# Strided attention: Q cast to bf16 on GpSimd and transposed in 32x32 blocks on VectorE, in place of TensorE transposes and ScalarE copies

## Chip, cores, metric

The kernel runs on one core of one Trainium2 chip. The metric is the device time of one execution in microseconds. Every kernel was run several times; medians are quoted with the lowest and highest run. All runs quoted were in the fast state. Ratios are the mean time of one kernel's fast runs over the mean of the other's fast runs of the same rounds, so not quite the ratio of the medians quoted beside them. The profile's span starts and ends inside the execution and is about 1.8 us shorter than the time (128.5 us for a run of 130.28).

## The reference

Shapes are batch 8, heads 12, sequence 1024, head size 64, float32. Every query attends only to the 16 keys and values at positions 0, 64, 128, ...:

```python
attend = np.arange(0, seq, stride)              # 16 positions
scores  = einsum('bhqd,bhkd->bhqk', q, K[:, :, attend]) / sqrt(64)
weights = exp(scores - max) ; weights /= weights.sum() + 1e-10
result  = einsum('bhqk,bhkd->bhqd', weights, V[:, :, attend])
```

There is little arithmetic. All of Q (25.2 MB) is read and an output of the same size is written; with the few rows of K and V that makes 51.12 MB of transfers.

## The kernel before

The 96 (batch, head) pairs are worked on in 24 groups of four. Per group: one 1 MB load of Q, 16 TensorE transposes, two ScalarE copies of the transposed Q to SBUF, four score matmuls that run side by side on 32 columns of the array each (four of about 0.39 us in 0.40 us together), two exps, eight small matmuls for the sums, a reciprocal, eight output matmuls, four VectorE products that normalise, one 1 MB store. Loads run up to 11 groups ahead.

```python
def transposes(g, x):                       # x = 0, 1
    ps = psum_qt.tile([P, 8, P], BF16, ...)
    for i in range(8):
        nc.tensor.transpose(ps[:, i], <high halves of qn[g], 128 columns>, identity)
    nc.scalar.copy(qt[g][:, x], ps)
def scores(g):
    for j in range(4):
        nc.tensor.matmul(sc[32*j:32*j+32], lhsT=kt[:, 32*j:32*j+32], rhs=<qt[g]>,
                         start=True, stop=True, tile_position=(0, 32*j))
    # ... two exps on ScalarE into w[g]
# ... sums(g): 8 matmuls and a reciprocal; outputs(g, c): 2 matmuls and a product
for g in range(NG):
    sums(g); outputs(g, 0); outputs(g, 1)
    if g + 1 < NG: scores(g + 1)
    outputs(g, 2)
    if g + 2 < NG: transposes(g + 2, 0)
    outputs(g, 3)
    if g + 2 < NG: transposes(g + 2, 1)
    store(g)
    if g + QBUFS < NG: load(g + QBUFS)      # QBUFS = 11
```

The softmax here doesn't subtract the row's maximum and nothing guards it: scores larger than these inputs give would overflow.

## Time and profile before

| | before |
|---|---|
| time, median of 3 (lowest, highest) | 130.45 us (130.32, 130.61) |
| DMA queue, share of 16 engines' span | 96.3% |
| bytes per group / measured rate | 2.1 MB / about 420 GB/s = 5.0 us |
| period of the compute loop | 3.93 us per group |
| last store issued | 114.3 us |

These are lines of the page of before: busy time by engine, the DMA row in 40 slices (tenths) with GB/s below it, the DMA queues (packets, MB, share of 16 engines), the chain that ended last, and the costliest groups of instructions (busy us, mean ns of one, idle before and its cause).

```profile
span 128.5 us, 2215 instructions
...
PE 69.4 (54%) x880; PEld 51.1 (40%) x880; DVE 83.7 (65%) x144; ACT 86.3 (67%) x103; POOL 5.1 (4%) x23
...
DMA  2999989999899899999999999999998999999980
GB/s 57 351 398 418 449 367 490 388 423 439 339 421 487 357 441 439 413 434 449 383 467 426 393 459 428 393 469 421 405 469 357 416 434 416 421 428 421 434 337 23
...
q1 hardware_dynamic: 7712, 51.12, 96.3%
q8 instruction: 7, 0.11, 0.4%
q14 instruction: 3, 0.02, 0.0%
...
ACT 60%; PE 13%; DVE 5%; DMA 3%; POOL 3%; issue 2%; ACTq 1%; DVEq 0%; POOLq 0%
...
L243 DVE TENSOR_TENSOR out_sb<-o_ps,rec 128x512 f32<-128x512 f32 x96 | 63.3, 688 | 15.3 <-PE o_ps L238 12.9
L198 ACT COPY qt<-qt_ps 128x1024 bf16<-128x1024 bf16 x48 | 46.2, 1015 | 5.2 <-PE qt_ps L193 4.7
L218 ACT ACTIVATE w<-sc 64x512 bf16<-64x512 f32 x48 | 35.4, 737 | 13.2 <-PE sc L206 12.9
...
L193 PE MATMUL qt_ps<-identity,qn 128*128 128x128 bf16 x384 | 30.7, 227 | 0.2 <-ACT qt L198 0.2
...
L206 PE MATMUL sc<-qt,k_t 128*32 128x512 bf16 x96 | 9.8, 395 | 24.5 <-ACT qt L198 24.5
...
```

The chain of waits names ScalarE, and it is right about the compute loop: copy, copy, score matmuls, exp, exp, one after the other. But that loop is not what ends the run. The DMA row reads 8 or 9 from the third slice to the third last. The queue of the sync engine tells how the run ends; the columns are who waited for what, total us, times, longest:

```profile
...
SPq L34 <- DVE out_sb L243: 20.0, 12, 3.3
...
SPq L307 <- DMA out_dram<-out_sb: 12.6, 1, 12.6
...
```

After the last store has been issued the kernel waits 12.6 us for stores to land.

The last microseconds in stretches (window, length, busy us of the engines with counts, TensorE clock, DMA share, GB/s):

```profile
...
core 0: us, PE busy (x) PEld busy (x) DVE busy (x) ACT busy (x) POOL busy (x), PEclk, DMA share, GB/s
...
90.00:110.00 20.00, 13.42 (x182) 9.83 (x179) 15.32 (x26) 17.33 (x21) 0.00 (x0) 1.00 1.00 418
...
118.00:122.00 4.00, 0.00 (x0) 0.00 (x0) 0.00 (x0) 0.00 (x0) 0.00 (x0) 0.50 1.01 426
...
124.00:125.00 1.00, 0.00 (x0) 0.00 (x0) 0.00 (x0) 0.00 (x0) 0.00 (x0) 0.50 0.61 254
125.00:126.00 1.00, 0.00 (x0) 0.00 (x0) 0.00 (x0) 0.00 (x0) 0.00 (x0) 0.50 0.26 107
...
```

### The profile page before, as it was taken

To read this page: it belongs to the slowest core of one execution; us is meant where nothing else is said; L and a number is where in the kernel's file an instruction comes from. 1 tells how busy PE (TensorE), PEld (TensorE's weight loads), DVE (VectorE), ACT (ScalarE), POOL (GpSimd) and SP (SyncE) were. 2 spreads that over 40 slices of the span, in tenths; PEclk is the share of its full clock that TensorE was granted. 3 is DMA by queue.
4 is the path that set the end of the run, shared out by engine and by line. 5 is a ranking of instruction groups with operands and counts; after the bars stand their busy time and mean duration, and the time that the engine had idled before them with its cause. 6 is when DMAs were issued, how large, how long until landed. Compare 5 with 4: busy or idle time off the path is not lost.

```text
span 128.5 us, 2215 instructions
## 1 busy us (share of the span) xinstructions
PE 69.4 (54%) x880; PEld 51.1 (40%) x880; DVE 83.7 (65%) x144; ACT 86.3 (67%) x103; POOL 5.1 (4%) x23
## 2 busy tenths in 40 slices
PE   0071665975656866558766578665687655510000
PEld 0040542754445654445544456443465444300000
DVE  6229963787677777787777877877877778750000
ACT  2163294988889888898888898888988888400000
POOL 4470000000000000000000000000000000000000
PEclk9999997799999999999999999999999999955555
DMA  2999989999899899999999999999998999999980
GB/s 57 351 398 418 449 367 490 388 423 439 339 421 487 357 441 439 413 434 449 383 467 426 393 459 428 393 469 421 405 469 357 416 434 416 421 428 421 434 337 23
DMA packets 7722, 51.26 MB, mean 399 GB/s; under 512 B 3872, under 2 KB 3872, under 8 KB 3872
## 3 DMA queue, kind: packets, MB, share of 16 engines
q1 hardware_dynamic: 7712, 51.12, 96.3%
q8 instruction: 7, 0.11, 0.4%
q14 instruction: 3, 0.02, 0.0%
HBM read 25.95 MB, written 25.17 MB: 398 GB/s over the span
## 4 chain that ended last, share of the span: by engine, by line
ACT 60%; PE 13%; DVE 5%; DMA 3%; POOL 3%; issue 2%; ACTq 1%; DVEq 0%; POOLq 0%
ACT qt L198 34%; ACT w L218 26%; PE sc L206 8%; DVE v_bd L180 3%; DMA k_raw<-in_K_dram 3%; PE qt_ps L193 2%; PE o_ps L238 2%; DVE out_sb L243 1%; POOL k_dup L116 1%; POOL perm_v L120 1%; PE sm L227 1%; POOL v_bf L124 1%; ACTq L307 1%; DVEq L307 0%; PE vp L175 0%
## 5 line engine op out<-in xcount | busy, mean ns | idle before, releaser
L243 DVE TENSOR_TENSOR out_sb<-o_ps,rec 128x512 f32<-128x512 f32 x96 | 63.3, 688 | 15.3 <-PE o_ps L238 12.9
L198 ACT COPY qt<-qt_ps 128x1024 bf16<-128x1024 bf16 x48 | 46.2, 1015 | 5.2 <-PE qt_ps L193 4.7
L218 ACT ACTIVATE w<-sc 64x512 bf16<-64x512 f32 x48 | 35.4, 737 | 13.2 <-PE sc L206 12.9
L238 PE MATMUL o_ps<-v_bd,w 128*128 128x256 bf16 x192 | 33.4, 278 | 0.6 <-DVE out_sb L243 0.6
L193 PE MATMUL qt_ps<-identity,qn 128*128 128x128 bf16 x384 | 30.7, 227 | 0.2 <-ACT qt L198 0.2
L193 PEld LDWEIGHTS <-qn 128*128 128x128 bf16 x384 | 27.0, 102 | 3.9 <-issue 2.6
L206 PE MATMUL sc<-qt,k_t 128*32 128x512 bf16 x96 | 9.8, 395 | 24.5 <-ACT qt L198 24.5
L238 PEld LDWEIGHTS <-w 128*128 128x128 bf16 x192 | 14.3, 98 | 6.9 <-issue 6.2
L206 PEld LDWEIGHTS <-k_t 128*32 128x32 bf16 x96 | 4.4, 93 | 29.3 <-issue 29.2
L231 DVE RECIPROCAL rec<-sm 128x32 f32<-128x32 f32 x24 | 8.6, 358 | 9.0 <-PE sm L227 9.0
L227 PE MATMUL sm<-s_sel,w 128*128 128x4 bf16 x192 | 8.5, 166 | 6.9 <-ACT w L218 6.9
L227 PEld LDWEIGHTS <-w 128*128 128x128 bf16 x192 | 6.4, 96 | 11.0 <-ACT w L218 11.0
L180 DVE TENSOR_SCALAR v_bd<-vp,mask 128x384 bf16<-128x384 f32 x16 | 8.5, 608 | 0.1
L166 ACT CAST k_t<-kp 64x512 bf16<-64x512 f32 x6 | 3.5, 579 | 3.6 <-PE kp L160 3.5
L160 PE MATMUL kp<-perm_k,k_dup 128*128 128x128 bf16 x12 | 1.5, 312 | 6.7 <-POOL k_dup L116 6.7
L175 PE MATMUL vp<-v_bf,perm_v 128*128 128x384 bf16 x4 | 1.8, 490 | 4.6 <-DVE v_bd L180 4.1
L160 PEld LDWEIGHTS <-k_dup 128*128 128x128 bf16 x12 | 1.2, 145 | 6.7 <-POOL k_dup L116 6.7
L138 DVE TENSOR_SCALAR slot_i<-iota_p 128x1 int16<-128x1 int16 x1 | 0.2, 156 | 4.7 <-POOL iota_p L136 4.7
L166 ACT ACT_TABLE_LOAD x1 | 1.3, 1283 | 2.5 <-DVE k_t L127 2.5
L127 DVE MEMSET k_t<- 128x1536 uint32 x1 | 1.3, 1338 | 1.1 <-PEq L293 1.1
L175 PEld LDWEIGHTS <-perm_v 128*128 128x128 bf16 x4 | 0.5, 127 | 3.7 <-issue 3.7
L116 POOL CAST k_dup<-k_raw 128x768 bf16<-128x768 f32 x2 | 1.6, 827 | 3.0 <-DMA k_raw<-in_K_dram 3.0
(15 smaller groups left out, 6.0 us busy)
## 6 DMA issues: line engine op xcount, KB each, us to landing
qn<-in_Q_dram SPq DMA_DIRECT2D x24, 1024.0 KB, 19.0
out_dram<-out_sb SPq DMA_DIRECT2D x24, 1024.0 KB, 19.5
k_raw<-in_K_dram SPq DMA_DIRECT2D x1, 384.0 KB, 4.3
v_raw<-in_V_dram SPq DMA_DIRECT2D x1, 384.0 KB, 5.4
```

The source lines that it names most:

```text
L116: nc.gpsimd.tensor_copy(out=k_dup[:, :, e], in_=k_raw)
L160: nc.tensor.matmul(kp[:, i], lhsT=k_dup[:, 4 * n + i].rearrange("p e d -> p (e d)"), rhs=pk, start=True, stop=True,)
L166: nc.scalar.copy(k_t[h, 4 * n : 4 * n + 4, :, :, e].rearrange("p n c s k -> p (n c s) k"), kp[h].rearrange("p n c s k -> p (n c s) k"),)
L180: nc.vector.tensor_scalar(out=v_bd[:, 6 * n : 6 * n + 6, c, s], in0=vp, scalar1=mask[:, s : s + 1], scalar2=None, op0=ALU.mult,)
L193: nc.tensor.transpose(ps[:, i], _ap_with(qb, [qb.ap[0], [2, P]], extra_offset=(8 * x + i) * 2 * P + 1), identity,)
L198: nc.scalar.copy(qt[g][:, x], ps)
L206: nc.tensor.matmul(sc[32 * j : 32 * j + 32], lhsT=kt[:, 32 * j : 32 * j + 32], rhs=_ap_with(q, [q.ap[0], [P, 8], [8 * P, 2], [1, 32]], ext ...
L218: nc.scalar.activation(out=_ap_with(wa, [wa.ap[0], [P, 8], [1, 2], [2, 32]], extra_offset=64 * a), in_=sc[64 * a : 64 * a + 64].rearrange( ...
L227: nc.tensor.matmul(sm[:, :, i], lhsT=wt[g][:, i], rhs=s_sel, start=True, stop=True)
L231: nc.vector.reciprocal(rec[g], sm.rearrange("p b i e -> p b (i e)"))
L238: nc.tensor.matmul(ps[:, :, i], lhsT=wt[g][:, 2 * c + i], rhs=v_bd[:, g // 2, g % 2].rearrange("p s d -> p (s d)"), start=True, stop=True,)
L243: nc.vector.tensor_tensor(out=out_sb[g][:, :, 4 * c : 4 * c + 4], in0=ps.rearrange("p b i (e d) -> p b (i e) d", e=2), in1=rec[g][:, :, 4 ...
```

## The change

The intent is to relieve TensorE and ScalarE. GpSimd casts Q to bf16; VectorE transposes it as 32x32 blocks of 32-bit words, each a pair of bf16 values; the scores then contract over (head, d pair) with the full height of the array, in four accumulating matmuls against keys set in zeros. The values are multiplied with a head mask per group on GpSimd, the keys are prepared in three portions, two of them inside the loop. K, Q0, V are loaded in that order, and the first two loads of Q have 128 rows of 8 KB in place of 32 of 32 KB.

```diff
-    QBUFS = 11
+    QBUFS = 10
-        _copy(nc, qn[g], <Q of group g in 32 rows>)
+        n = P if g < 2 else 32
+        _copy(nc, qn[g], <Q of group g in n rows>)
 # ... K, V, Q0, Q1 ... becomes K, Q0, V, Q1 ...
-    nc.vector.memset(k_t, 0.0)
+    nc.vector.memset(k_t[:, 0:8], 0.0)
+    nc.gpsimd.memset(k_t[:, 8:NG], 0.0)
-    def transposes(g, x): ...            # 8 PE transposes, 1 ScalarE copy, twice per group
+    def cast(g):
+        nc.gpsimd.tensor_copy(out=qb[g], in_=qn[g])
+    def transpose(g):
+        nc.vector.transpose(qt[g].bitcast(I32), qb[g].bitcast(I32))
+    def values(g):
+        nc.gpsimd.tensor_tensor(out=vb[g], in0=mask, in1=<v_rep>, op=ALU.mult)
     def scores(g):
-        for j in range(4): matmul(sc[32*j:32*j+32], ..., tile_position=(0, 32*j))
+        for e in range(2):
+            for f in range(2):
+                nc.tensor.matmul(sc, lhsT=k_t[:, g, f, NK*(1-e):NK*(1-e)+P],
+                                 rhs=<qt[g], every second column>, start=e+f == 0, stop=e+f == 2)
+    keys(0); cast(0); transpose(0); scores(0); value_rows(); values(0)
+    cast(1); transpose(1); values(1); cast(2)
     for g in range(NG):
+        if g + 2 < NG: transpose(g + 2)
         sums(g) ... outputs(g, 3)        # scores(g + 1) stays between outputs 1 and 2
+        if g + 2 < NG: values(g + 2)
+        if g + 3 < NG: cast(g + 3)
+        if g in (2, 4): keys(g // 2)
         store(g)
 # ... cuts: tiles and pools, keys(), value_rows(), set-up
```

More of the change, by code (lines that the diff above doesn't have):

```diff
@@ L14 @@
 I16 = mybir.dt.int16
+I32 = mybir.dt.int32
 AF = mybir.ActivationFunctionType
@@ L68 @@
     SD = S * D
+    KW = P + NK
     assert B * H == NG * HG and S == 1024 and D == 64 and NK == 16
-    QBUFS = 11
+    QBUFS = 10
     OBUFS = 9
@@ L75 @@
     out_pool = ctx.enter_context(tc.tile_pool(name="outsb", bufs=OBUFS))
+    qb_pool = ctx.enter_context(tc.tile_pool(name="qb", bufs=2))
     qt_pool = ctx.enter_context(tc.tile_pool(name="qt", bufs=2))
+    vb_pool = ctx.enter_context(tc.tile_pool(name="vb", bufs=3))
     rec_pool = ctx.enter_context(tc.tile_pool(name="rec", bufs=2))
-    psum_qt = ctx.enter_context(tc.tile_pool(name="pqt", bufs=2, space=bass.MemoryType.PSUM))
     psum_sc = ctx.enter_context(tc.tile_pool(name="psc", bufs=2, space=bass.MemoryType.PSUM))
-    psum_o = ctx.enter_context(tc.tile_pool(name="po", bufs=3, space=bass.MemoryType.PSUM))
-    psum_s = ctx.enter_context(tc.tile_pool(name="psm", bufs=1, space=bass.MemoryType.PSUM))
+    psum_o = ctx.enter_context(tc.tile_pool(name="po", bufs=4, space=bass.MemoryType.PSUM))
+    psum_s = ctx.enter_context(tc.tile_pool(name="psm", bufs=2, space=bass.MemoryType.PSUM))
     ctx.enter_context(tc.manual_schedule())
@@ L88 @@
     kv_src = [[stride * D, P], [2 * HG * SD, NC], [1, D]]
-    nc.sync.dma_start(k_raw, _ap_with(K, kv_src))
-    nc.sync.dma_start(v_raw, _ap_with(V, kv_src))
     qn = {}
@@ L95, in load @@
         qn[g] = qn_pool.tile([P, 32 * D], FP32, name="qn", tag="qn")
-        _copy(
-            nc, qn[g], _ap_with(Q, [[HG * SD // 32, 32], [1, HG * SD // 32]], g * HG * SD)
-        )
-    for g in range(QBUFS):
+        n = P if g < 2 else 32
+        _copy(nc, qn[g], _ap_with(Q, [[HG * SD // n, n], [1, HG * SD // n]], g * HG * SD))
+    nc.sync.dma_start(k_raw, _ap_with(K, kv_src))
+    load(0)
+    nc.sync.dma_start(v_raw, _ap_with(V, kv_src))
+    for g in range(1, QBUFS):
         load(g)
@@ L110 @@
     perm_v = const.tile([P, 2, 2, 2, 2, NK], BF16, name="perm_v")
+    iota_p = const.tile([P, 1], I16, name="iota_p")
+    nc.gpsimd.iota(iota_p, pattern=[[0, 1]], base=0, channel_multiplier=1)
+    col4 = const.tile([P, 4], I16, name="col4")
+    nc.gpsimd.iota(col4, pattern=[[1, 4]], base=0, channel_multiplier=0)
     for c in range(2):
@@ L113 @@
             nc.gpsimd.tensor_copy(out=perm_k[:, c, a], in_=id_v[:, c, :, a])
-    k_dup = const.tile([P, NC, 2, D], BF16, name="k_dup")
-    for e in range(2):
-        nc.gpsimd.tensor_copy(out=k_dup[:, :, e], in_=k_raw)
     for c in range(2):
@@ L122 @@
                 )
-    v_bf = const.tile([P, NC, D], BF16, name="v_bf")
-    nc.gpsimd.tensor_copy(out=v_bf, in_=v_raw)
-    k_t = const.tile([P, NC, 2, 4, 2, NK], BF16, name="k_t")
-    nc.vector.memset(k_t, 0.0)
+    k_t = const.tile([P, NG, 2, KW], BF16, name="k_t")
+    nc.vector.memset(k_t[:, 0:8], 0.0)
     w_bufs = []
@@ L132 @@
         w_bufs.append(w)
-    iota_p = const.tile([P, 1], I16, name="iota_p")
-    nc.gpsimd.iota(iota_p, pattern=[[0, 1]], base=0, channel_multiplier=1)
+    nc.gpsimd.memset(k_t[:, 8:NG], 0.0)
     slot_i = const.tile([P, 1], I16, name="slot_i")
@@ L143 @@
     nc.vector.tensor_copy(out=slot_f, in_=slot_i)
-    col4 = const.tile([P, 4], I16, name="col4")
-    nc.gpsimd.iota(col4, pattern=[[1, 4]], base=0, channel_multiplier=0)
     s_sel = const.tile([P, 4], BF16, name="s_sel")
@@ L149 @@
     )
-    mask = const.tile([P, 4], FP32, name="mask")
-    nc.vector.tensor_scalar(
-        out=mask, in0=col4, scalar1=slot_f, scalar2=None, op0=ALU.is_equal
-    )
-    pk = perm_k.rearrange("p c a b k -> p (c a b k)")
-    for n in range(NC // 4):
-        kp = psum_o.tile([P, 4, 2, 4, NK], FP32, name="kp", tag="o")
-        for i in range(4):
-            nc.tensor.matmul(
-                kp[:, i], lhsT=k_dup[:, 4 * n + i].rearrange("p e d -> p (e d)"),
-                rhs=pk, start=True, stop=True,
-            )
-        for e in range(2):
-            h = slice(64 * e, 64 * e + 64)
+    slot_m = const.tile([P, 4], FP32, name="slot_m")
@@ new lines, with keys @@
+    nc.vector.tensor_copy(out=slot_m, in_=s_sel)
+    mask = const.tile([P, 4, D], BF16, name="mask")
+    nc.vector.tensor_copy(out=mask, in_=s_sel.unsqueeze(2).to_broadcast([P, 4, D]))
+    k_m = const.tile([P, NC, 2, 4, 32], BF16, name="k_m")
+    v_bf = const.tile([P, NC, D], BF16, name="v_bf")
+    v_rep = const.tile([P, NC, 2, D], BF16, name="v_rep")
+    def keys(m):
+        kr = k_raw[:, 4 * m : 4 * m + 4].rearrange("p n (q f) -> p n f q", f=2)
+        for h in range(4):
+            nc.vector.tensor_scalar(
+                out=k_m[:, 4 * m : 4 * m + 4, :, h], in0=kr,
+                scalar1=slot_m[:, h : h + 1], scalar2=None, op0=ALU.mult,
+            )
+        for u in range(2):
+            kp = psum_o.tile([P, 2, 2, 2, 4 * NK], FP32, name="kp", tag="o")
+            for i in range(2):
+                for f in range(2):
+                    nc.tensor.matmul(
+                        kp[:, i, :, f],
+                        lhsT=k_m[:, 4 * m + 2 * u + i, f].rearrange("p h q -> p (h q)"),
+                        rhs=perm_k.rearrange("p c a b k -> p c (a b k)"),
+                        start=True, stop=True,
+                    )
+            g0 = 8 * m + 4 * u
+            dst = k_t[:, g0 : g0 + 4]
@@ L166 @@
             nc.scalar.copy(
-                k_t[h, 4 * n : 4 * n + 4, :, :, e].rearrange("p n c s k -> p (n c s) k"),
-                kp[h].rearrange("p n c s k -> p (n c s) k"),
-            )
-    v_bd = const.tile([P, NC, 2, 4, D], BF16, name="v_bd")
-    for n in range(2):
-        for c in range(2):
-            vp = psum_sc.tile([P, NC // 2, D], FP32, name="vp", tag="sc")
-            nc.tensor.matmul(
-                vp, lhsT=perm_v[:, c].rearrange("p a b e k -> p (a b e k)"),
-                rhs=v_bf[:, 6 * n : 6 * n + 6], start=True, stop=True,
-            )
-            for s in range(4):
-                nc.vector.tensor_scalar(
-                    out=v_bd[:, 6 * n : 6 * n + 6, c, s], in0=vp,
-                    scalar1=mask[:, s : s + 1], scalar2=None, op0=ALU.mult,
-                )
@@ L185 @@
-    qt, wt, rec, out_sb = {}, {}, {}, {}
-    def transposes(g, x):
-        if x == 0:
-            qt[g] = qt_pool.tile([P, 2, 8, P], BF16, name="qt", tag="qt")
-        ps = psum_qt.tile([P, 8, P], BF16, name="qt_ps", tag="qt_ps")
-        qb = qn[g].bitcast(BF16)
-        for i in range(8):
-            nc.tensor.transpose(
-                ps[:, i],
-                _ap_with(qb, [qb.ap[0], [2, P]], extra_offset=(8 * x + i) * 2 * P + 1),
-                identity,
-            )
-        nc.scalar.copy(qt[g][:, x], ps)
+                _ap_with(dst, [dst.ap[0], [KW, 8], [32, 4], [1, NK]], extra_offset=NK),
@@ new lines, in keys, with value_rows @@
+                kp.rearrange("p i c f (s k) -> p (i c f) s k", s=4),
+            )
+    def value_rows():
+        nc.vector.tensor_copy(out=v_bf, in_=v_raw)
+        for n in range(2):
+            for c in range(2):
+                vp = psum_sc.tile([P, NC // 2, D], FP32, name="vp", tag="sc")
+                nc.tensor.matmul(
+                    vp, lhsT=perm_v[:, c].rearrange("p a b e k -> p (a b e k)"),
+                    rhs=v_bf[:, 6 * n : 6 * n + 6], start=True, stop=True,
+                )
+                nc.vector.tensor_copy(out=v_rep[:, 6 * n : 6 * n + 6, c], in_=vp)
@@ new lines @@
+    qb, qt, wt, vb, rec, out_sb = {}, {}, {}, {}, {}, {}
+    def values(g):
+        vb[g] = vb_pool.tile([P, 4, D], BF16, name="vb", tag="vb")
+        nc.gpsimd.tensor_tensor(
+            out=vb[g], in0=mask,
+            in1=v_rep[:, g // 2, g % 2].unsqueeze(1).to_broadcast([P, 4, D]),
+            op=ALU.mult,
+        )
+    def cast(g):
+        qb[g] = qb_pool.tile([P, 32 * D], BF16, name="qb", tag="qb")
+        nc.gpsimd.tensor_copy(out=qb[g], in_=qn[g])
+    def transpose(g):
+        qt[g] = qt_pool.tile([P, 32 * D], BF16, name="qt", tag="qt")
+        nc.vector.transpose(qt[g].bitcast(I32), qb[g].bitcast(I32))
@@ L202, in scores @@
         q = qt[g]
-        kt = k_t[:, g // 2, g % 2].rearrange("p s e k -> p (s e k)")
-        for j in range(4):
-            a, b = divmod(j, 2)
-            nc.tensor.matmul(
-                sc[32 * j : 32 * j + 32],
-                lhsT=kt[:, 32 * j : 32 * j + 32],
-                rhs=_ap_with(
-                    q, [q.ap[0], [P, 8], [8 * P, 2], [1, 32]],
-                    extra_offset=32 * (2 * b + a),
-                ),
-                start=True, stop=True, tile_position=(0, 32 * j),
-            )
+        for e in range(2):
+            for f in range(2):
+                nc.tensor.matmul(
+                    sc, lhsT=k_t[:, g, f, NK * (1 - e) : NK * (1 - e) + P],
+                    rhs=_ap_with(
+                        q, [q.ap[0], [2 * D, 8], [16 * D, 2], [2, 32]],
+                        extra_offset=D * e + f,
+                    ),
+                    start=e + f == 0, stop=e + f == 2,
+                )
         w = wt[g] = w_bufs[g % 3]
@@ L239, in outputs @@
                 ps[:, :, i], lhsT=wt[g][:, 2 * c + i],
-                rhs=v_bd[:, g // 2, g % 2].rearrange("p s d -> p (s d)"),
+                rhs=vb[g].rearrange("p s d -> p (s d)"),
                 start=True, stop=True,
@@ L256, in store @@
         )
-    for g in range(2):
-        for x in range(2):
-            transposes(g, x)
+    keys(0)
+    cast(0)
+    transpose(0)
     scores(0)
+    value_rows()
+    values(0)
+    cast(1)
+    transpose(1)
+    values(1)
+    cast(2)
     for g in range(NG):
+        if g + 2 < NG:
+            transpose(g + 2)
         sums(g)
@@ L268 @@
         outputs(g, 2)
-        if g + 2 < NG:
-            transposes(g + 2, 0)
         outputs(g, 3)
         if g + 2 < NG:
-            transposes(g + 2, 1)
+            values(g + 2)
+        if g + 3 < NG:
+            cast(g + 3)
+        if g in (2, 4):
+            keys(g // 2)
         store(g)
```

## The prediction

> **What bounds the kernel now.** The transfers. The page's DMA row reads 9 tenths from the third slice to the third last; the hardware DMA queue is busy for 96.3% of the 128.5 us span while moving 51.12 MB, and the table of windows shows DMA share 0.99 to 1.03 and 418 to 434 GB/s from 28 us to 124 us. Idle: the first 2.3 us and the last 2. The chain of waits names ScalarE instead (qt copy 34%, exp 26%): that is the compute loop, which steps every 3.93 us per group of four heads (qt copies 1.94, score matmuls 0.42, exps 1.49). But a group moves 2.1 MB, which at 420 GB/s takes 5.0 us. So the loop is faster. It ends at 114.2 us and the last 12.6 us are a wait for stores to drain.
>
> **What the change does, per group.**
> - TensorE loses 16 transposes (about 1.2 us) and gains a full-height score: four serial 512-column matmuls, [...]in place of four concurrent ones (0.40).
> - ScalarE loses the two qt copies (1.94) and keeps 1.49 of exp.
> - GpSimd gains the cast of 128x2048. The 128x768 cast took 827 ns, so an estimate is 2.2 us[...].
> - VectorE gains one block transpose of 128x1024 32-bit pairs. [...]With the reciprocal (0.36) and four products (2.48 together when nothing holds them, as at the end of before) VectorE has about 4.1 us per group and becomes the loop's limit.
> - Setup shrinks: the first store should be issued near 16 to 17 us in place of 25.2.
>
> **Contention.** [...]I expect little; the products should stay at 0.69 us.
>
> **On the critical path.** Almost nothing. Bytes and packets are the same (two loads become 8 KB packets). The new loop, some 4.1 to 4.4 us, is still under the 5.0 of the transfers and starts 8 us earlier, so compute ends near 112 to 120 us and the rest drains. One Q buffer less matters little. Gains can come only from small dips of the DMA between 20 and 28 us (share 0.93), half a microsecond at most.
>
> **Prediction:** 130.2 us, 8 in 10 between 129.0 and 132.3. Chances: faster by over 2% 0.05, within 2% 0.82, slower by over 2% 0.13.
>
> **What would show it.** DMA busy 95 to 97%, windows between 30 and 120 us at 415 to 430 GB/s; [...]cast near 2.2 us; products 0.69 us; ScalarE busy about 40 us, VectorE about 105 us; the first store near 16 us; the chain of waits passing to VectorE and DMA; final wait for stores 8 to 14 us.
>
> **What would make it wrong.** If the loop's period exceeds about 4.5 us ([...]casts and VectorE blocking one another), compute ends after 125 us, the DMA runs dry and the time becomes period times 24 plus about 20: 139 us at 4.9. It would be faster only if the transfers themselves became faster, which I don't expect.

To follow the forecast's sums: VectorE came to about 4.1 us per group, and the loop's 4.1 to 4.4 us and VectorE's 105 us rest on it. Its terms 0.36 and 2.48 us are from the trace of before.

## The result, and the profile after

| | before | after |
|---|---|---|
| time, median of 4 (lowest, highest) | 130.38 us (130.2, 130.61) | 129.76 us (129.49, 129.87) |
| ratio, 95% interval | | 0.9948 (0.9926 to 0.997) |
| first store issued | 25.2 us | 23.6 us |
| last store issued | 114.3 us | 120.0 us |
| TensorE instructions in the program | 1,762 | 1,018 |

The change gains half a percent (the interval lies below 1, and well within 2%). This is the page after, with the same kinds of lines:

```profile
span 127.7 us, 1518 instructions
...
PE 73.3 (57%) x508; PEld 38.6 (30%) x508; DVE 109.2 (85%) x170; ACT 39.6 (31%) x55; POOL 66.7 (52%) x69
...
DMA  2999989898998998989989999999999999999981
GB/s 70 380 322 459 482 339 482 349 482 359 462 472 336 503 400 377 505 346 431 493 344 439 454 385 436 441 408 452 426 398 464 385 421 431 426 416 428 421 372 46
...
q1 hardware_dynamic: 7904, 51.12, 96.8%
q8 instruction: 4, 0.07, 0.2%
q14 instruction: 5, 0.04, 0.1%
...
DVE 2%; DVEq 0%; issue 0%
...
L254 DVE TENSOR_TENSOR out_sb<-o_ps,rec 128x512 f32<-128x512 f32 x96 | 59.9, 685 | 4.8 <-PE o_ps L249 2.6
L229 ACT ACTIVATE w<-sc 64x512 bf16<-64x512 f32 x48 | 35.1, 732 | 60.0 <-PE sc L218 56.7
L207 POOL CAST qb<-qn 128x2048 bf16<-128x2048 f32 x24 | 45.5, 1898 | 0.4 <-DMA qn<-in_Q_dram 0.4
...
L199 POOL TENSOR_TENSOR vb<-mask,v_rep 128x256 bf16<-128x256 bf16 x24 | 16.1, 670 | 40.3 <-PE o_ps L249 35.4
L218 PE MATMUL sc<-qt,k_t 128*128 128x512 bf16 x96 | 32.7, 472 | 1.5 <-DVE qt L211 1.2
L211 DVE STREAM_TRANSPOSE qt<-qb 128x1024 int32<-128x1024 int32 x24 | 29.7, 1237 | 1.6 <-POOL qb L207 1.6
...
```

Compare the first lines: ScalarE falls from 86.3 to 39.6 us, VectorE rises from 83.7 to 109.2, GpSimd from 5.1 to 66.7. The DMA queue moves the same 51.12 MB in nearly the same share. The qt copies (46.2 us on ScalarE) are gone; block transpose (1,237 ns), cast (1,898 ns) and value product (670 ns) are new, and the normalising product on VectorE stays at 685 ns (688 before). The chain of waits no longer names a loop at all: it ends after a few pieces. One more line differs: q8 carries 4 packets in place of 7.

```profile
...
SPq L35 <- DVE out_sb L254: 74.5, 22, 9.4
...
SPq L328 <- DMA out_dram<-out_sb: 6.1, 1, 6.1
...
```

The sync engine now waits 74.5 us for VectorE's output, against 20.0 before, and the final wait for stores has shrunk from 12.6 to 6.1 us. Compute ends later than before, and still the run is shorter.

```profile
...
90.00:110.00 20.00, 13.90 (x102) 7.25 (x101) 19.55 (x31) 7.33 (x10) 10.69 (x9) 0.83 1.00 420
...
118.00:122.00 4.00, 0.00 (x0) 0.00 (x0) 1.98 (x4) 0.00 (x0) 0.00 (x0) 0.59 1.02 424
...
124.00:125.00 1.00, 0.00 (x0) 0.00 (x0) 0.00 (x0) 0.00 (x0) 0.00 (x0) 0.50 0.45 188
125.00:126.00 1.00, 0.00 (x0) 0.00 (x0) 0.00 (x0) 0.00 (x0) 0.00 (x0) 0.50 0.18 74
...
```

Up to 122 us the rates are those of before (420 against 418, 424 against 426 GB/s). Then they part: shares of 0.45 and 0.18 where before had 0.61 and 0.26. To see why, take the completion records of the last store. The packed trace has 16 of them for every transfer, as many as the page counts DMA engines. I read each as the landing of one engine's part, though the records name no engine; what is said below of single engines rests on that reading. No view of `prof` lists these times, so they were read from the file. For the last store they are, in us after the first of the 16 (first and last in us from the span's start):

```
         first at                                  16 landings of the last store                            last at
before   124.21   0.00 0.04 0.04 0.07 0.35 0.47 0.84 0.93 1.36 1.67 1.73 1.76 1.84 1.89 2.35 3.29           127.50
after    124.15   0.00 0.04 0.14 0.15 0.15 0.26 0.29 0.35 0.76 1.04 1.35 1.48 1.66 1.83 2.45 2.55           126.70
```

The first engine is done at the same time in both (0.06 us apart). The last is done 0.80 us earlier after the change, and the span is 0.78 us shorter. So the gain lies in how unevenly the engines finish. In before, the 16 landings of each transfer stay within 0.6 us up to 27 us. The first of the 16 KB instruction packets starts at 27.2 us, and the next transfer to land (first engine at 28.6 us) has one engine 1.92 us late, the others still within 0.5. More engines fall back one by one from then on. Count the engines that land more than 1.3 us after the first: from the transfer before to the transfer after each of the seven packets the count rises by exactly one (to 1, 2, 3, 4, 6, 7 and 8; one more rise, from 4 to 5, comes without a packet), and it never falls.

That gave the theory for the half microsecond. The q8 lines show 7 and 4 packets of 16 KB; the TensorE programs have 1,762 and 1,018 instructions, so 252 and 255 to a packet. That they are fetches of TensorE's program was my reading; the records don't name the engine that they serve, but in runs 7 to 9 their count follows the length of that program (0, 6 and 13). Theory: each fetch (one packet of 16 KB) holds up one of the 16 engines, and where transfers bound the kernel the unluckiest engine ends it. Rivals: the start of the transfers (their new order and shape), or the pace at which compute now releases loads and stores.

### The profile page after: what moved, and what is told of

Its sections match the earlier page's. It is cut to its first block, busy times and chain, and to the rows that moved or that the text cites. A ratio compares the mean times of both kernels' runs of the same rounds, so it can differ in the third digit from the quotient of the medians.

```text
span 127.7 us, 1518 instructions
## 1 busy us (share of the span) xinstructions
PE 73.3 (57%) x508; PEld 38.6 (30%) x508; DVE 109.2 (85%) x170; ACT 39.6 (31%) x55; POOL 66.7 (52%) x69
## 3 DMA queue, kind: packets, MB, share of 16 engines
q1 hardware_dynamic: 7904, 51.12, 96.8%
## 5 line engine op out<-in xcount | busy, mean ns | idle before, releaser
L254 DVE TENSOR_TENSOR out_sb<-o_ps,rec 128x512 f32<-128x512 f32 x96 | 59.9, 685 | 4.8 <-PE o_ps L249 2.6
L207 POOL CAST qb<-qn 128x2048 bf16<-128x2048 f32 x24 | 45.5, 1898 | 0.4 <-DMA qn<-in_Q_dram 0.4
L249 PE MATMUL o_ps<-vb,w 128*128 128x256 bf16 x192 | 38.0, 321 | 2.4 <-DVE out_sb L254 1.4
L199 POOL TENSOR_TENSOR vb<-mask,v_rep 128x256 bf16<-128x256 bf16 x24 | 16.1, 670 | 40.3 <-PE o_ps L249 35.4
L218 PE MATMUL sc<-qt,k_t 128*128 128x512 bf16 x96 | 32.7, 472 | 1.5 <-DVE qt L211 1.2
L211 DVE STREAM_TRANSPOSE qt<-qb 128x1024 int32<-128x1024 int32 x24 | 29.7, 1237 | 1.6 <-POOL qb L207 1.6
L249 PEld LDWEIGHTS <-w 128*128 128x128 bf16 x192 | 19.3, 110 | 16.2 <-issue 8.6
L238 PEld LDWEIGHTS <-w 128*128 128x128 bf16 x192 | 6.9, 100 | 30.1 <-ACT w L229 29.6
L218 PEld LDWEIGHTS <-k_t 128*128 128x128 bf16 x96 | 10.8, 114 | 12.0 <-issue 6.5
L161 DVE TENSOR_SCALAR k_m<-k_raw,slot_m 128x256 bf16<-128x256 f32 x12 | 6.8, 626 | 0.0
L135 POOL MEMSET k_t<- 128x4608 bf16 x1 | 3.9, 3938 | 0.0
L129 DVE MEMSET k_t<- 128x1152 uint32 x1 | 1.0, 1018 | 1.0 <-PEq L314 1.0
```

What stands on the lines that cost most here:

```text
L161: nc.vector.tensor_scalar(out=k_m[:, 4 * m : 4 * m + 4, :, h], in0=kr, scalar1=slot_m[:, h : h + 1], scalar2=None, op0=ALU.mult,)
L199: nc.gpsimd.tensor_tensor(out=vb[g], in0=mask, in1=v_rep[:, g // 2, g % 2].unsqueeze(1).to_broadcast([P, 4, D]), op=ALU.mult,)
L207: nc.gpsimd.tensor_copy(out=qb[g], in_=qn[g])
L211: nc.vector.transpose(qt[g].bitcast(I32), qb[g].bitcast(I32))
L218: nc.tensor.matmul(sc, lhsT=k_t[:, g, f, NK * (1 - e) : NK * (1 - e) + P], rhs=_ap_with(q, [q.ap[0], [2 * D, 8], [16 * D, 2], [2, 32]], ex ...
L238: nc.tensor.matmul(sm[:, :, i], lhsT=wt[g][:, i], rhs=s_sel, start=True, stop=True)
```

## Experiments

Kernels that were run together shared a chip and its runs of before; medians of before lay between 130.29 and 130.52 us.

### 1. Transfers alone

```diff
-    <all compute>
+    o = const.tile(...); nc.vector.memset(o, 0.0)      # stored for every group
     for g in range(NG):
         store(g)
         if g + QBUFS < NG: load(g + QBUFS)
```

> All compute is taken out (wrong result on purpose); the loads and stores of the changed kernel stay, in the same order and shapes. Theory (the transfers set the time of both kernels): 128.5 to 129.8 us, DMA share at least 96%. Rival (the compute loop still paces the transfers): clearly shorter, below 126 us.

Measured: 128.49 us (128.1 to 128.84), ratio to before 0.9851 (0.9832 to 0.987), DMA 97.0%. Result wrong, as intended. The time is at the lower edge of the range. The transfers alone need nearly all of the time of both kernels. One of its 16 engines was late by 2.21 us at the end and the other 15 lay within 0.6, though no instruction was fetched while it ran (its page lists no instruction ring). One engine was already 1.38 us late in the first load, and the last engine's lag went from 1.34 to 2.18 us at about 41 us. So fetches are not the only cause of a late engine; this other cause is not known.

### 2. The start of the transfers, given to the kernel before

```diff
-    nc.sync.dma_start(k_raw, ...); nc.sync.dma_start(v_raw, ...)
-    for g in range(QBUFS): load(g)                     # 32 rows each
+    nc.sync.dma_start(k_raw, ...); load(0); nc.sync.dma_start(v_raw, ...)
+    for g in range(1, QBUFS): load(g)                  # 128 rows where g < 2
```

> The kernel before, with only the changed kernel's order of the first loads (K, Q0, V, Q1...) and the 128-row form of the first two Q loads. If the half microsecond comes from the start of the transfers: 129.6 to 130.0. If it comes from the loop (mix of loads and stores, or the end): 130.2 to 130.5, no change.

Measured: 130.7 us (130.17 to 130.86), ratio 1.0025 (1.0012 to 1.0039): no gain, but a loss of 0.25% that neither range allowed for.

### 3. The old start of the transfers, given to the changed kernel

```diff
-        n = P if g < 2 else 32
+        n = 32
 # ... and K, V, Q0, Q1 in the old order
```

> The changed kernel with the old order of first loads (K, V, Q0...) and the old 32-row form. If the half microsecond comes from the start of the transfers: 130.2 to 130.5. If it comes from the loop: 129.6 to 129.9.

Measured: 129.58 us (129.47 to 129.75), ratio 0.9946 (0.9934 to 0.9958), the same as the changed kernel. Runs 2 and 3 together: order and shape of the first loads are not the cause. The one Q buffer less (QBUFS 10 for 11) was not tested by itself.

### 4. Without the blocked compare in the set-up

In the changed kernel a slot compare on 128x4 elements, s_sel, takes 3.15 us on VectorE (0.23 in before). The timeline (start us, length us, instruction, idle before) shows it stuck until a GpSimd memset of the key tile ends at 7.15 us, and what delays group 0 after that:

```profile
...
3.21 3.94 POOL L135 MEMSET k_t<- 128x4608 bf16 x1
...
4.01 3.15 DVE L145 TENSOR_SCALAR s_sel<-col,slot_f 128x4 bf16<-128x4 int16 x1
...
7.54 2.04 POOL L207 CAST qb<-qn 128x2048 bf16<-128x2048 f32 x1 [0.39 <-DMA qn<-in_Q_dram]
...
15.85 0.40 PE L238 MATMUL sm<-s_sel,w 128*128 128x4 bf16 x8
...
17.02 1.25 DVE L211 STREAM_TRANSPOSE qt<-qb 128x1024 int32<-128x1024 int32 x1 [0.37 <-POOL qb L207]
...
19.48 1.25 DVE L211 STREAM_TRANSPOSE qt<-qb 128x1024 int32<-128x1024 int32 x1 [1.22 <-POOL qb L207]
...
20.65 0.32 DVE L242 RECIPROCAL rec<-sm 128x32 f32<-128x32 f32 x1
```

```diff
-    nc.gpsimd.memset(k_t[:, 8:NG], 0.0)
     cast(0)
+    nc.gpsimd.memset(<k_t[:, 8:NG] as 32-bit words>, 0)
     transpose(0)
```

> The changed kernel with the GpSimd memset of the key tile halved (as 32-bit words) and moved behind the first cast. Contention theory: the 128x4 slot compare on VectorE falls from 3.16 us to about 0.25, and the first store is issued about 3 us earlier than 23.6, near 20.5. Theory that transfers set the time: still 129.5 to 130.0. Rival (the start of compute is on the path): 127 to 128.5.

Measured: the compare fell to 228 ns, so the memset had blocked it. But the first store was issued at 22.9 us, only 0.7 earlier, and not 3 us as I had written: the first cast still started at 7.68 us, when Q0 had landed. The rest is in the timeline above. The sums of group 0 are started at 15.85 and take 0.40 us, but the reciprocal that uses them starts at 20.65, behind the block transposes of groups 1 and 2, which come first in VectorE's program and wait for their casts. Time 130.08 us (130.0 to 130.25), ratio 0.9983 (0.9971 to 0.9995): just over the range, and not faster than the changed kernel, but 0.3 us slower than its 129.76 (0.5 slower than run 3). Its fetches are the same in number (4 of 16 KB), and so are the engines more than 1.3 us late at the end (6), but its last engine is 3.12 us behind the first, against 2.55. So the number of fetches alone doesn't give the spread. Which engine a fetch lands on, and whether one is hit twice, would matter too, but the trace doesn't name the engine; this part stays argued.

### 5. More TensorE instructions in the changed kernel

```diff
-        for i in range(8):
+        for i in [*range(8)] * 3:
             nc.tensor.matmul(sm[:, :, i], lhsT=wt[g][:, i], rhs=s_sel, ...)
```

> The changed kernel with the eight small sum matmuls of each group issued three times (same result): TensorE's program grows from 1,018 to 1,786 instructions, about as long as before's 1,762; VectorE, the loads and the stores are untouched. Theory (fetching the instruction stream takes time from single DMA engines, and the slowest engine ends the run): the 16 KB fetches rise from 4 to 7, the spread of the last store's 16 landings from 2.6 us to 3.0 to 3.6, time 130.0 to 130.6. Rival (the half microsecond comes from the pace at which loads and stores are issued): 129.5 to 129.9.

Measured: 130.81 us (130.72 to 132.25), ratio 1.0054 (1.0023 to 1.0086), 7 fetches of 16 KB. The time is over the range and the landings are not as expected: the spread of the last store was 1.40 us, not 3.0 to 3.6, and its first landing came at 126.66 us, not near 124.2 as in before and the changed kernel. The extra matmuls delayed compute, the last store went out at 122.6 us in place of 120.0, and the DMA rate fell to 340 GB/s in the fourth last of the 40 slices. So two things changed at once, and about the time the run decides nothing. Its trace does speak for the fetch theory: in the transfer that landed from 114.3 us on, before the rate fell, 8 engines were more than 1.3 us late and the spread was 3.75 us (in the changed kernel at that time 5 and 2.61, in before 8 and 3.33). In the transfer from 121.0 us on only one was, as in run 10, where the engines catch up when they run out of work.

### 6. Fewer TensorE instructions in the kernel before

```diff
-        for i in range(8):
+        for i in range(1):
             nc.tensor.transpose(ps[:, i], ...)
-        nc.scalar.copy(qt[g][:, x], ps)
+        nc.scalar.copy(qt[g][:, x], ps[:, 0:1].to_broadcast([P, 8, P]))
```

> The kernel before with one transpose in eight kept (wrong result on purpose): 1,090 TensorE instructions in place of 1,762; ScalarE's copies and exps, which pace the loop, keep their sizes. Fetch theory: 4 fetches in place of 7, spread of the last store's landings 2.2 to 2.8 us in place of 3.3, time 129.5 to 129.9. Rival (pace or mix of loads and stores): no change, 130.1 to 130.5.

Measured: 129.83 us (129.66 to 130.01), ratio 0.9958 (0.9946 to 0.997), 4 fetches of 16 KB, spread 2.80 us, 6 engines more than 1.3 us late as in the changed kernel, in place of 8. Time, fetches and spread are as the fetch theory said. It is not clean proof, since the loop also slowed (last store at 117.7 us instead of 114.3), so the pace rival was not shut out.

### 7 to 9. Program length alone

Since runs 5 and 6 each moved compute too, the dose was given to transfers without compute. Per group, k small matmuls read the loaded Q tile; nothing uses their result.

```diff
 # transfers alone, and
     for g in range(NG):
+        for i in range(k):                              # k = 1, 36, 73
+            nc.tensor.matmul(ps, lhsT=<128 columns of qn[g]>, rhs=r, start=True, stop=True)
         store(g)
```

> Only loads, stores and one small matmul per group that reads the Q tile (wrong result on purpose; 50 TensorE instructions in all). Both theories: no instruction fetches while the transfers run, 128.2 to 128.9 us, the last store's 16 landings spread over about 2.2 us, all but one of them within 0.7.

> The same with 36 small matmuls per group: 1,730 TensorE instructions, as long a program as before's, and no other compute. Theory (instruction fetches delay single DMA engines): 6 or 7 fetches of 16 KB, several of the 16 landings late by 1 to 2 us or more, spread 2.6 to 3.8 us, time 0.4 to 1.3 us above the run with one matmul per group. Rival (instruction fetches cost nothing): within 0.2 us of it, same pattern of landings.

> The same with 73 small matmuls per group: 3,506 TensorE instructions. Fetch theory: 13 or 14 fetches, nearly every one of the 16 landings late, time 0.8 to 2.0 us above the run with one matmul per group. Rival: within 0.2 us of it.

| TensorE instructions | 16 KB fetches | time, median (lowest, highest) | ratio to before | first / last landing of the last store |
|---|---|---|---|---|
| 50 | 0 | 127.7 us (127.6, 128.19) | 0.9802 | 123.98 / 124.97 us |
| 1,730 | 6 | 129.94 us (129.14, 130.11) | 0.9955 | 124.07 / 127.06 us |
| 3,506 | 13 | 131.95 us (131.11, 132.21) | 1.0098 | 124.00 / 129.45 us |

The fetch lines of the second and third of these:

```profile
...
q8 instruction: 6, 0.10, 0.3%
...
```

```profile
...
q8 instruction: 13, 0.21, 0.6%
...
```

The 16 landings of the last store, us after the first:

```
k = 1    0.00 0.04 0.06 0.07 0.10 0.33 0.34 0.38 0.39 0.43 0.47 0.51 0.52 0.56 0.65 0.99
k = 36   0.00 0.05 0.05 0.09 0.19 0.23 0.30 0.30 0.56 1.41 1.55 1.79 1.81 1.83 1.91 2.99
k = 73   0.00 0.05 0.10 0.20 0.32 0.37 0.39 1.41 1.97 1.98 2.98 2.99 3.06 3.18 3.22 5.46
```

The first landing stays at 124.0 to 124.1 us in all three; the last moves by 2.1 and 4.5 us, and the time by 2.2 and 4.3. The late engines stand in steps, about 1.4 to 2.0, about 3.0 to 3.2, and 5.5 us, as if hit once, twice or more. The time rises by 2.24/6 = 0.37 and 4.25/13 = 0.33 us per fetch. (From run 1 as the start, on another chip and with its one late engine, it would be 0.24 and 0.27.) The rise is more than both ranges I had set (0.4 to 1.3 and 0.8 to 2.0 us): the direction was as the theory said, the size larger. The run with k = 1 was also below its range, since its last engine was 0.99 us late in place of the 2.2 of run 1. The rival, that fetches cost nothing, is out. With the fetches the matmuls that read SBUF grew too. The trace speaks against those as the cause: with k = 36 matmuls run for every group, but the engines more than 1.3 us late go from 0 to 1, to 2 and to 3 exactly in the first transfer after each of the first three fetches (18.3, 27.1 and 36.7 us), and stay put between them (7 at the end, after six). Nor did the sync engine wait for TensorE in the runs with k = 36 and 73.

### 10. A slower VectorE loop

```diff
         nc.vector.reciprocal(rec[g], ...)
+        nc.vector.reciprocal(rec[g], ...)
```

> The changed kernel with every reciprocal on VectorE done twice, about 0.33 us more per group. The compute loop goes from 3.98 to about 4.3 us and its last store from 120.0 to about 127.5 us. Theory (compute of the changed kernel has only some 4 us to spare under the transfers): the transfers run dry at the end and the time rises to 131.5 to 133.5. Rival (compute has plenty to spare, as the loop of 3.98 us against 5.0 of the transfers suggests): below 130.3.

Measured: 134.3 us (133.25 to 135.22), ratio 1.0326 (1.0276 to 1.0375): over the range, and the rival is out. The last store was issued at 126.2 us in the profiled run, of 133.25 us; the DMA rate over the last slices shows the transfers running dry:

```profile
...
GB/s 76 366 331 474 429 439 379 459 429 356 419 496 356 426 486 399 401 496 391 394 498 389 394 503 384 394 508 376 394 503 339 421 429 396 351 257 184 329 331 202
...
```

In this run the last store's landings lie within 0.17 us of each other: when the engines wait for work, the late ones catch up. A third of a microsecond per group, on an engine with 15% idle time, made the changed kernel 3% slower than before.

### 11 and 12. Both kernels with three stores in four left out

```diff
-        store(g)
+        if g % 4 == 3: store(g)
```

> The kernel before with only every fourth group stored (wrong result on purpose), so that the transfers no longer bound it; what is left is the compute path. Theory: compute ends at the same 114 us, the last store drains alone: 118 to 121 us.

> The changed kernel with only every fourth group stored (wrong result on purpose). Theory (the change made the compute path longer, and the transfers hide it): compute ends near 120 us, time 123 to 126 us, that is slower than the thinned kernel before by 4 to 6 us. Rival (the change relieved compute, as its aim was): faster than the thinned kernel before.

Measured: 121.37 us (121.34, 121.41) for before and 126.16 us (125.28, 127.05) for the changed kernel; both slightly over their ranges, at the expected distance (4.8 us). Last stores were issued at 114.5 and 120.2 us, as in the full kernels (columns: shortest, median and longest issue in ns, first and last start in us):

```profile
...
L34 SPq DMA_DIRECT2D out_dram<-out_sb x6: 539/592/624, 36.5 to 114.5; - x6
...
```

```profile
...
L35 SPq DMA_DIRECT2D out_dram<-out_sb x6: 538/592/623, 38.9 to 120.2; - x6
...
```

So where transfers no longer bound the kernels, the changed one is the slower. The change did not relieve compute as a whole; it moved the load from ScalarE to VectorE and lengthened the path.

## Why the prediction was right or wrong, point by point

- **Right: the transfers set the time, so the change does little.** Predicted 130.2 us, measured 129.76. Transfers alone took 128.49 us (run 1). The small size is no luck; that the gain came near the "half a microsecond at most" is, since its place was wrong (last point).
- **Right: most costs.** Block transpose 1.24 us, products 0.685 us (0.69), ScalarE 39.6 us (40), VectorE 109.2 us (105), DMA 96.8%. GpSimd's cast was mis-sized, 1.90 us for 2.2: I scaled the 827 ns of 128x768 in proportion. The two measured sizes would fit 0.19 us per instruction and 0.83 ns per element (an estimate from these two points alone).
- **Right in the loop, incomplete in the set-up: contention.** Products and transposes don't change while GpSimd works: all products took 680 to 693 ns and all transposes 1,230 to 1,247 ns, and after GpSimd's last instruction had ended at 108.05 us a transpose still took 1.24 us and four products 2.48 us together, as at 60 to 68 us. But in the set-up a compare that before runs in 0.23 us was blocked for 3.15 us (run 4), which the prediction did not look for.
- **Wrong: "the first store should be issued near 16 to 17 us in place of 25.2".** It came at 23.6 us. I added up durations and left out the order on VectorE: group 0's reciprocal stands behind two transposes that wait for casts, from 16.25 to 20.65 us.
- **Wrong: "final wait for stores 8 to 14 us".** It was 6.1. Besides the late start, the two portions of keys inside the loop were not costed: stores 3.98 us apart otherwise are 7.24 and 7.38 us apart there (31.56 to 38.80 and 42.78 to 50.16 us), so 6.7 us in all. The last store was issued at 120.0 us, at the edge of "112 to 120": partly luck, as the loop itself was a little faster than forecast (3.98 us against 4.1 to 4.4).
- **Too generous: "if the loop's period exceeds about 4.5 us".** That bound rested on the early start. Run 10, with about 0.33 us more per group and so an estimated 4.3, was 3% slower than before; the prediction's "period times 24 plus about 20" would give 123 us there, and 134.3 were measured. The half percent stood a third of a microsecond per group from a loss.
- **Wrong: "Gains can come only from small dips of the DMA between 20 and 28 us".** Those dips stayed (share 0.94 and 0.95, against 0.94 and 0.93). The gain lies at the end: 0.73 of the 0.78 us of span is a smaller spread of the 16 engines (2.55 against 3.29 us). That fetches of TensorE's instructions cause such spreads is shown by runs 7 to 9. That they make engines late in these kernels rests on the traces: in before one more late engine after each of its seven fetches, and at the end 8 or 9 late engines in the kernels with 7 fetches (before, run 2) against 6 in the four with 4 that stayed bound by transfers (the changed kernel, runs 3, 4 and 6). How late the last one is follows the count less closely. By 0.33 to 0.37 us per fetch, three fewer would be worth 1.0 to 1.1 us (estimate from runs 8 and 9; 0.7 to 0.8 from run 1 as the start); measured was 0.6. The changed kernel also has five packets of 8 KB on the other instruction ring in place of three, whose part was not tested, and run 4 shows that the same count can give a spread 0.57 us larger. How much of the half microsecond is count and how much is luck of which engine is hit stays open.

## What to carry to other kernels

When the DMA row is full from end to end, work out the time of bytes over rate first and ask of a compute change only how far it stays below that: here it took away 47 us of ScalarE work and made the compute path 6 us longer, and neither moved the time much. Look at how the last transfer lands on its 16 engines, not only at the mean DMA share: a ring that took 0.3% of the engines' time (6 fetches, run 8) cost 2.2 us, because fetches made engines late (0, then 1, 2 and 3 of 16 after the first three, 7 at the end) and, as long as the queue stayed full, late engines stayed late (in before the count never fell; in run 10, where the queue ran dry, the last landings lay within 0.17 us). In these transfer-bound runs a shorter TensorE program was worth something in itself, about a third of a microsecond per 16 KB fetch.
